# Nine start offsets, 16 bytes apart, for the weight tiles of a two-layer retention and gMLP kernel

## Chip, cores and metric

The kernel runs on one core of one Trainium2 chip. The metric is device time in microseconds of one execution: 906.26 us, the median of three runs of the kernel before (906.09 to 908.04).

## What is computed

Two layers over 512 latent tokens and 256 context tokens, width 1024, all in float32. Layer 0 is a bidirectional multi-scale retention mixer: 4 heads with q and k of 256 and v and z of 512 columns each. Layer 1 is a chunked gMLP with spatial gating: u, v and z of 2048 columns, then an output projection. The latent stream leaves through a final RMSNorm.

```python
def retention_project(h, w_in):
    q = to_heads(h @ w_in[:, :a], RET_HEADS)
    k = to_heads(h @ w_in[:, a:bq], RET_HEADS) * (RET_QK_DIM ** -0.5)
    v = to_heads(h @ w_in[:, bq:cq], RET_HEADS)
    z = h @ w_in[:, cq:]
...
def gmlp_chunk_mixer(h, w_in, vnorm_g, w_s, b_s, w_out):
    u = h @ w_in[:, :GM_WIDTH]
    v = (h @ w_in[:, GM_WIDTH:2 * GM_WIDTH]).astype(F32)
    z = h @ w_in[:, 2 * GM_WIDTH:]
    ...
    y = u * mixed.reshape(b, l, w).astype(u.dtype)
    return (y * jax.nn.silu(z)) @ w_out
```

The change concerns the products `h @ w_in` of both layers and the gMLP's output product.

## The kernel before

**Halves.** Each float32 operand of a large product is split into a high half (the value cast to the type float32r) and a low half (the rest), and a product is three matmuls: low by high, high by low, high by high (`mm3`, L126). `split` (L132) makes the halves: ScalarE casts the high half, VectorE subtracts it from the source for the low half.

**Quads.** A weight block is cut into four quarters, a quad, and the product of a quad takes seven quarter products instead of eight (Strassen-Winograd), with sums of quarters on both sides. `Stream` (L155) holds the list of weight tiles in the order in which they are used. Its `upto` (L195) prepares the next tile two ahead of its use: it takes raw quarters (128 x 1024, loaded by DMA), subtracts where the name begins with T, and splits the result into a tile of halves. `get` hands it to the product.

**Tiles of halves.** `hl_tile` (L110) deals four slots, `hl0` to `hl3`, in turn. A slot is 2080 floats wide, and a tile of halves uses 2048 of them: 1024 of the high half, then 1024 of the low one. The 32 floats (128 bytes) that are left over let a tile begin at byte 0 or at byte 128 of its slot. The rule before is the line

```python
        o = 32 if moves != (i % 2 == 1) else 0
```

where `i` is the slot and `moves` is true for the quads "vz" and "v1". In the program's memory map the slots begin at bytes 138560, 169408, 177728 and 186048 of a partition; modulo 256 that is 64, 192, 64 and 192. So before the change every tile of halves of the quads "kq" and "u", of "o" and of `load_wo` begins at 64 modulo 256, and every tile of "vz" and "v1" at 192. The activations' tiles (`oA..`, `oS..`, `hc`) begin at multiples of 256, and the pieces that a matmul reads lie at multiples of 512 bytes within any of the tiles.

**Two kinds of product.** `features` (L312; quads "kq" and "u") has the weights' halves as the stationary operand and the activations as the moving one, 256 columns; `tokens` (L320; "vz" and "v1") has the activations stationary and the weights' halves moving, 256 columns. `out1` (L1231; blocks "o") has `ya` or `yb` stationary and the weights' halves moving, 512 columns. A quarter product is 24 matmuls; a layer-0 quad is 9 quarter products (seven, and two of the context tokens), a "v1" or "u" quad 7, an "o" block one tile of 24 matmuls.

**Order.** `QUADS` (L255) goes kq 0; vz (0,0) and vz (0,1) side by side; vz (1,0), vz (1,1), kq 1, vz (2,0), vz (2,1), kq 2, vz (3,0), kq 3, vz (3,1). Then come four heads of attention, whose output weights are split by `load_wo` (L873), the four "v1" quads in two pairs, and the eight "u" quads with four "o" blocks behind each of u2, u4, u6 and u7. Two "v1" tiles (the first of v1 0 and of v1 1) are put into the free tiles `oA22` and `oS2` by `place_at` (L273), and bear the name `hl_e` in the trace; they don't pass through `hl_tile`. The order on each engine is the order of the text (`Queue`, with few exceptions); loads are issued by SyncE when a raw slot comes free.

Of the kernel before, what the change touches and what calls it, by code (L numbers as in the profile page):

```python
# [67 lines left out]
def hybrid_kernel(ctx, tc, xT_d, cT_d, cv_d, sv_d, rows_d, ada0_d, adag_d, w_d, rope_d, dec_d, ws_d, id_d, out_d):  # L68
# [13 lines left out]
    def st(shape, tag, dt=F32, bufs=1, name=None):  # L82
        return sb.tile(shape, dt, tag=tag, name=name or tag, bufs=bufs)
# [23 lines left out]
    lay({"w0": 4096, "w1": 4096, "w2": 4096, "w3": 4096, "w7": 4096, "g0": 4096, "g1": 4096, "dec": 4 * TW})  # L107
    hls = [0]

    def hl_tile(moves=False):  # L110

        i = hls[0] % HL
        hls[0] += 1
        t = st([P, 2080], f"hl{i}", F32R, name="hl")
        o = 32 if moves != (i % 2 == 1) else 0
        return t[:, o:o + 2048].rearrange("p (a n) -> p a n", a=2)

    def t2(name, shape=(P, 512), dt=F32):
# [13 lines left out]
    def split(hl, src, late=None):  # L132
        h, l = hl
        act.copy(h, src)
        low = lambda: dve.tensor_tensor(l, src, f32(h), ALU.subtract)
        if late is None:
            low()
        else:
            late.append(low)
# [15 lines left out]
    class Stream:  # L155
# [3 lines left out]
        def __init__(self):  # L159
            self.items, self.loads, self.raws, self.left, self.tiles = [], [], {}, {}, {}  # L160
            self.free, self.stage, self.done, self.sent, self.at = [], 0, 0, 0, -1
            self.gate = self.limit = self.cap = None

        def quad(self, q, names, place=None):
            for name in names:
                self.item(q, name, place)
# [28 lines left out]
        def upto(self, n, late=None):  # L195

            while self.done < min(n, self.limit or len(self.items)):
                q, name, uses, at, place = self.items[self.done]
                self.pump()
                raw = lambda u: self.raws[q, u]  # L200
                r = raw(at)
                if name[0] == "T":
                    dve.tensor_tensor(r, raw(uses[0]), raw(uses[1]), ALU.subtract)
                elif name[0] == "gated":
                    g = self.gate[:, name[1]:name[1] + 512].unsqueeze(1).to_broadcast([P, 2, 512])
                    rr = r.rearrange("p (e n) -> p e n", e=2)
                    dve.tensor_tensor(rr, rr, g, ALU.mult)
                hl = place() if place else hl_tile(q[0] in ("vz", "v1"))
                split((hl[:, 0, :], hl[:, 1, :]), r, late)
                self.tiles[self.done] = hl  # L210
                self.done += 1
                if late is None:
                    self.drop(q, uses)
                else:
                    late.append(lambda: self.drop(q, uses))
# [657 lines left out]
    def load_wo(h):  # L873
        raws = []
        for c in range(4):
            for j in range(len(raws), min(c + 2, 4)):
                raws.append(st([P, 1024], ("w0", "w7")[j % 2], name="raw"))
                load(raws[j], w_d[16 * h + 12 + j])
            if c == 0:
                yield  # L880
            w = hl_tile()
            split((w[:, 0, :], w[:, 1, :]), raws[c])
            wos.setdefault(h, []).append(w)
            yield
# [556 lines left out]
```

## Time and profile before

| what | value |
|---|---|
| three timed runs, us | 906.09, 906.26, 908.04 |
| profiled execution: its span, us (no other time of it is given) | 908.2 |
| mean granted TensorE clock | 0.992 |
| busy TensorE (matmul) / weight load | 884.4 us (97%) / 839.3 us (92%) |
| busy VectorE / ScalarE / GpSimd | 720.0 us (79%) / 445.8 us (49%) / 51.4 us (6%) |
| DMA | 153.81 MB, mean 169 GB/s |

The span is the time from the first to the last instruction of the one execution that was traced. In a row of the timeline stand the start and the length in us, the engine, the operation, its output and inputs by their names in the program, the shape, and how many instructions are merged into the row. Matmuls overlap in the pipeline: a matmul of 256 columns is shown with 0.28 us, but the next one starts after about 0.12 us. The pace, the distance between two starts, is therefore a row's length less the length of one matmul, divided by the count less one.

### The profile page before, as it was taken

To read this page: it belongs to the slowest core of one execution; us is meant where nothing else is said; L and a number is where in the kernel's file an instruction comes from. 1 tells how busy PE (TensorE), PEld (TensorE's weight loads), DVE (VectorE), ACT (ScalarE), POOL (GpSimd) and SP (SyncE) were. 2 spreads that over 40 slices of the span, in tenths; PEclk is the share of its full clock that TensorE was granted. 3 is DMA by queue.
4 is the path that set the end of the run, shared out by engine and by line. 5 is a ranking of instruction groups with operands and counts; after the bars stand their busy time and mean duration, and the time that the engine had idled before them with its cause. 6 is when DMAs were issued, how large, how long until landed. Compare 5 with 4: busy or idle time off the path is not lost.

```text
span 908.2 us, 16915 instructions
## 1 busy us (share of the span) xinstructions
PE 884.4 (97%) x6872; PEld 839.3 (92%) x6872; DVE 720.0 (79%) x1024; ACT 445.8 (49%) x683; POOL 51.4 (6%) x88
## 2 busy tenths in 40 slices
PE   8999999999999999999999999999999999999986
PEld 7899999999999999998989898999999899899875
DVE  3689967698689876888677669999899478689975
ACT  5564634434445435626263558654445444353334
POOL 0001201101101011000000001111000000000000
PEclk9999999999999999999999999999999999999999
DMA  9933957467477458758253611636335035128002
GB/s 338 399 121 109 320 194 255 153 191 223 154 237 239 140 183 316 255 161 260 79 184 118 209 47 59 215 96 211 118 117 187 24 116 187 44 96 283 19 24 93
DMA packets 76782, 153.81 MB, mean 169 GB/s; under 512 B 7840, under 2 KB 34592, under 8 KB 76704
## 3 DMA queue, kind: packets, MB, share of 16 engines
q1 hardware_dynamic: 69840, 130.70, 44.2%
q0 software_dynamic: 6720, 22.03, 6.4%
q8 instruction: 54, 0.88, 0.4%
q14 instruction: 24, 0.20, 0.1%
q10 hardware_dynamic: 144, 0.01, 0.0%
HBM read 128.58 MB, written 24.12 MB: 168 GB/s over the span
## 4 chain that ended last, share of the span: by engine, by line
PE 67%; DVE 19%; DMA 5%; ACT 4%; issue 4%; SPq 1%; DVEq 0%; ACTq 0%
PE pst L54 67%; DVE hl L54 6%; DMA raw<-in_w_dram 3%; DVE raw L54 3%; DVE ya L54 2%; DVE o L54 2%; DVE snap L54 1%; SPq L54 1%; DMA vt<-vt 1%; DMA xq<-in_xT_dram 1%; ACT hl L54 1%; DVE f L54 1%; DVE pf L54 1%; ACT junk L54 1%; DVE oS L54 1%
## 5 line engine op out<-in xcount | busy, mean ns | idle before, releaser
L54 DVE TENSOR_TENSOR hl<-raw,hl 128x1024 fp32r<-128x1024 f32 x195 | 236.0, 1219 | 68.0 <-ACT hl L54 67.8
L54 ACT CAST hl<-raw 128x1024 fp32r<-128x1024 f32 x195 | 203.7, 1050 | 129.0 <-PE pst L54 71.2
L54 PE MATMUL pst<-oS,hl 128*128 128x256 f32 x1104 | 135.6, 282 | 4.6 <-DVE hl L54 3.9
L54 PE MATMUL pst<-hl,oS 128*128 128x256 f32 x1152 | 137.8, 281 | 2.0 <-DVE hl L54 1.8
L54 PEld LDWEIGHTS pst<-hl,oS 128*128 128x128 f32 x1152 | 135.8, 190 | 3.5 <-DVE hl L54 2.3
L54 PEld LDWEIGHTS pst<-oS,hl 128*128 128x128 f32 x1104 | 131.4, 190 | 6.9 <-ACT ya L54 3.7
L54 PE MATMUL pst<-oA,hl 128*128 128x256 f32 x936 | 117.5, 281 | 0.7 <-DVE snap L54 0.5
L54 PEld LDWEIGHTS pst<-oA,hl 128*128 128x128 f32 x936 | 112.2, 189 | 3.2 <-issue 1.3
L54 DVE TENSOR_TENSOR raw<-raw 128x1024 f32<-128x1024 f32 x92 | 111.4, 1218 | 1.2 <-DMA raw<-in_w_dram 0.5
L54 ACT COPY snap<-pst 128x512 f32<-128x512 f32 x92 | 53.9, 586 | 103.4 <-PE pst L54 102.9
L54 PE MATMUL pst<-hl,oA 128*128 128x256 f32 x816 | 98.6, 279 | 0.4 <-DVE snap L54 0.4
L54 PEld LDWEIGHTS pst<-hl,oA 128*128 128x128 f32 x816 | 96.3, 189 | 0.6 <-issue 0.6
L54 PE MATMUL pst<-og,hl 128*128 128x256 f32 x768 | 92.5, 281 | 0.0
L54 PEld LDWEIGHTS pst<-og,hl 128*128 128x128 f32 x768 | 90.4, 189 | 0.9 <-DVE acc L54 0.2
L54 PE MATMUL pst<-hl,ya 128*128 128x512 f32 x288 | 70.8, 399 | 2.7 <-DVE ya L54 2.7
L54 PEld LDWEIGHTS pst<-hl,ya 128*128 128x128 f32 x288 | 54.9, 192 | 15.2 <-DVE ya L54 3.1
L54 PE MATMUL pst<-v,ph 128*128 128x512 f32 x192 | 60.1, 395 | 0.0
L54 DVE TENSOR_TENSOR snap<-pst,snap 128x512 f32<-128x512 f32 x69 | 47.2, 684 | 3.9 <-PE pst L54 3.6
L54 ACT CAST ph<-pf 128x512 fp32r<-128x512 f32 x24 | 14.9, 621 | 67.1 <-DVE pf L54 66.7
L54 PE MATMUL pst<-hl,hc 128*128 128x256 f32 x384 | 47.4, 280 | 0.0
L54 PEld LDWEIGHTS pst<-hl,hc 128*128 128x128 f32 x384 | 46.0, 189 | 0.0
L54 PEld LDWEIGHTS pst<-v,ph 128*128 128x128 f32 x192 | 36.2, 188 | 7.3
(171 smaller groups left out, 970.3 us busy)
## 6 DMA issues: line engine op xcount, KB each, us to landing
raw<-in_w_dram SPq DMA_DIRECT2D x224, 256.0 KB, 4.4
bg<-in_adag_dram SPq DMA_DIRECT2D x32, 512.0 KB, 4.3
ada_w<-in_ada_dram SPq DMA_DIRECT2D x16, 512.0 KB, 8.7
raw<-in_w_dram SPq DMA_DIRECT2D x16, 512.0 KB, 4.3
bg<-in_dec_dram SPq DMA_DIRECT2D x12, 512.0 KB, 4.4
v<-snap POOLq DMA_DIRECT2D x16, 256.0 KB, 5.0
z<-snap POOLq DMA_DIRECT2D x16, 256.0 KB, 4.2
v<-v SPq DMA_DIRECT2D x8, 512.0 KB, 4.3
```

What stands on the lines that cost most here:

```text
L54: made = op(*args, **kw)
```

## The change

`hl_tile` takes another argument, `spread`. Where it is given, the tile begins at `4 * spread % 36` floats into its slot, whatever the slot: 0, 16, 32, 48, 64, 80, 96, 112 or 128 bytes, and then from 0 again. `Stream` numbers the quads and the "o" blocks in the order in which their first tile is prepared (`turn`), and `upto` gives that number. `load_wo` calls `hl_tile` as before, and its tiles and the two `hl_e` tiles keep their places. Kinds, numbers and order of the instructions on each engine are those of before; the addresses alone differ.

```diff
-    def hl_tile(moves=False):
+    def hl_tile(moves=False, spread=None):
...
-        o = 32 if moves != (i % 2 == 1) else 0
+        o = 4 * spread % 36 if spread is not None else 32 if moves != (i % 2 == 1) else 0
...
+            self.turns = {}
+
+        def turn(self, q):
+
+            if q not in self.turns:
+                self.turns[q] = len(self.turns)
+            return self.turns[q]
...
-                hl = place() if place else hl_tile(q[0] in ("vz", "v1"))
+                hl = place() if place else hl_tile(q[0] in ("vz", "v1"), self.turn(q))
```

This gives, by turn:

| quads or blocks in order | bytes into the slot |
|---|---|
| kq 0, vz (0,0), vz (0,1), vz (1,0), vz (1,1), kq 1 | 0, 16, 32, 48, 64, 80 |
| vz (2,0), vz (2,1), kq 2, vz (3,0), kq 3, vz (3,1) | 96, 112, 128, 0, 16, 32 |
| v1 0, v1 1, v1 2, v1 3 | 48, 64, 80, 96 |
| u0, u1, u2, four o | 112, 128, 0, then 16, 32, 48, 64 |
| u3, u4, four o | 80, 96, then 112, 128, 0, 16 |
| u5, u6, four o | 32, 48, then 64, 80, 96, 112 |
| u7, four o | 128, then 0, 16, 32, 48 |

Since the slots begin at 64 or 192 modulo 256 in turn, and the offset no longer evens that out, tiles of one quad now lie at two places modulo 256, 128 bytes apart.

## Prediction

> **What bounds the kernel now.** I read the page's busy line first, then the busy time by stage, then the rows of the timeline in which one kind of matmul runs without a gap.
>
> ```profile
> PE   884.4 (97%) x6872; PEld 839.3 (92%) x6872; DVE 720.0 (79%) x1024; ACT 445.8 (49%) x683; POOL 51.4 (6%) x88
> ```
> ```profile
> 59.80:164.40 104.60, 104.60 (x891) 104.60 (x889) 91.08 (x110) 56.48 (x76) 16.47 (x25) 1.00 0.60 198
> 164.40:345.60 181.20, 179.43 (x1514) 175.73 (x1513) 145.30 (x176) 79.42 (x102) 20.50 (x34) 0.99 0.62 200
> 345.60:550.50 204.90, 202.69 (x1442) 187.69 (x1441) 150.66 (x234) 105.58 (x180) 3.43 (x6) 1.00 0.53 170
> ...
> 558.90:631.50 72.60, 71.95 (x627) 71.36 (x626) 71.22 (x97) 42.01 (x56) 10.07 (x19) 1.00 0.53 177
> 631.50:699.00 67.50, 65.51 (x552) 65.34 (x551) 60.65 (x87) 35.08 (x49) 0.54 (x1) 0.97 0.42 137
> 699.00:908.00 209.00, 197.26 (x1309) 179.48 (x1307) 160.32 (x222) 87.01 (x129) 0.00 (x0) 0.98 0.30 99
> ```
>
> The columns of the second fence are the stretch, its length, then busy time and count of PE, PEld, DVE, ACT and POOL, the granted clock, and DMA. The stages are: the rest of the layer-0 quads up to 345.6 us (at 161.6 begins kq 1), attention, the "v1" quads from 558.9, and the "u" quads and "o" blocks from 631.5. TensorE is busy for 104.60 of 104.60 us, 179.43 of 181.20 and 71.95 of 72.60: in the quads nothing but the pace of the matmuls sets the time. In "v1" VectorE is busy for 71.22 of 72.60 us as well. In the last two stretches the chain that ended last goes through VectorE and DMA too, and TensorE has some 14 us of idle.
>
> A busy TensorE says little; the pace does. These are timeline rows of gapless matmuls:
>
> ```profile
> 84.78 20.42 PE L54 MATMUL pst<-hl,oS 128*128 128x256 f32 x172
> ```
> ```profile
> 285.76 5.60 PE L54 MATMUL pst<-hl,oS 128*128 128x256 f32 x48
> ```
> ```profile
> 550.51 3.04 PE L54 MATMUL pst<-hl_e,oA 128*128 128x256 f32 x24
> ```
> ```profile
> 554.18 3.11 PE L54 MATMUL pst<-hl_e,oA 128*128 128x256 f32 x24
> ```
> ```profile
> 709.82 6.34 PE L54 MATMUL pst<-hl,ya 128*128 128x512 f32 x27
> ```
> ```profile
> 7.93 1.04 PE L54 MATMUL pst<-ident,xq 128*128 128x128 f32 x8
> ```
>
> With one matmul taking 0.28 us (0.39 at 512 columns, 0.27 for the 128-column transposes), the paces are (20.42 - 0.28)/171 = **117.8 ns**, (5.60 - 0.28)/47 = **113.3 ns**, (3.04 - 0.28)/23 = **120.0 ns** and for the second such product (3.11 - 0.28)/23 = 123.0, (6.34 - 0.39)/26 = **228.8 ns** and (1.04 - 0.27)/7 = **110 ns**. The first two rows are the same work at the same start addresses, modulo 256 (weights' halves moving at 192, activations stationary at 0): one stretch goes at 117.8 and another at 113.3, and along the timeline a stretch keeps its pace until TensorE next waits. So there are two steady paces for one arrangement. The third and fourth rows are the only place before where the moving tile and the stationary tile begin at the same place modulo 256 (`hl_e` in `oA22`, `oA11`, both 0), and it goes at 120.0 or more. That is what the change touches: the start of one operand against that of the other. The transposes load 128 columns and move 128; their 110 ns is about what loading alone takes.
>
> **The change part by part.** *Instructions.* None is added, removed or moved, and no wait. The DMAs and their order are the same.
>
> *Writing the tiles.* ScalarE and VectorE write the halves at the new places.
>
> ```profile
> L54 DVE TENSOR_TENSOR hl<-raw,hl 128x1024 fp32r<-128x1024 f32 x195 | 236.0, 1219 | 68.0 <-ACT hl L54 67.8
> L54 ACT CAST hl<-raw 128x1024 fp32r<-128x1024 f32 x195 | 203.7, 1050 | 129.0 <-PE pst L54 71.2
> ...
> L54 DVE TENSOR_TENSOR raw<-raw 128x1024 f32<-128x1024 f32 x92 | 111.4, 1218 | 1.2 <-DMA raw<-in_w_dram 0.5
> ```
>
> The 195 subtractions into slots at two offsets take 1219 ns, those of the raw tiles at quite other places 1218. I take nothing. The trace has no start that is not a multiple of 64 bytes, so this is bounded only by such rows; if each took 2% more, 24 ns by the 179 tiles concerned is 4 us of VectorE, hidden under TensorE except in "v1", where 26 tiles make 0.6 us. A gain I exclude: equal durations at all the present places show nothing left to win.
>
> *Reading the tiles: the term that decides.* By the table of turns, 8 of the 11 layer-0 quads after kq 0 begin off a multiple of 64 (16, 32, 48, 80, 96, 112, 16, 32): 8 x 216 = 1728 matmuls. Of "v1" it is three quads, 3 x 168 less one `hl_e` tile, 480; of "u" five quads (112, 80, 96, 32, 48), 840; of "o" 11 of 16 blocks, 264 matmuls of 512 columns. With offset 64 the tiles in the odd slots begin at 192 + 64 = 256, in step with the other operand, as in the `hl_e` row: some 120 matmuls. That is about 3170 matmuls of 256 columns in a relation that the trace shows at 120.0 or not at all. Bounds from rows: below, 110 ns, where the moving stream costs nothing beside the load; above, an estimate: if an operand is fetched in pieces of 64 bytes, 1024 moved bytes touch 17 pieces instead of 16, and 113.3 x 17/16 = 120.4; 512 loaded bytes touch 9 instead of 8, and 110 x 9/8 = 124. I take **120.0**, the one row in which the relation of the two starts is another than 64 bytes apart; the end of 124 stays for the range.
>
> *The sum*, by stage:
> - vz (0,0), (0,1), (1,0) and half of (1,1), now at 117.8: 750 x 2.2 ns = 1.7 us.
> - turns 5 to 11, of which five quads are off 64: now at either pace, midpoint 115.6: 1080 x 4.4 = 4.8 us. Both on the path (PE 104.60 of 104.60; 179.43 of 181.20).
> - "v1": now at 113.3 nearly throughout. 71.95 us of matmuls of TensorE against 71.22 of VectorE; a slower TensorE leaves VectorE behind it. 510 x 6.7 = 3.4 us.
> - "u": 840 x 4.4 = 3.7, and "o": 264 by an assumed 4.5 ns = 1.2. I count half, 2.5 us, since TensorE waits here for others, and the slower matmuls eat into those waits:
>
> ```profile
> PE pst L54 <- DVE hl L54: 3.9, 3, 2.0
> PE pst L54 <- DVE ya L54: 2.7, 1, 2.7
> PE pst L54 <- DVE snap L54: 0.5, 1, 0.5
> ```
>
> Together 12.4 us. The span becomes 908.2 + 12.4 = 920.6; it lies 1.9 us over the median of the timed runs, so the time is 906.26 + 12.4 = **918.6 us**, +1.4%.
>
> *Clock.* After one wait of TensorE the same 24 matmuls take 4.48 us instead of 2.88 (granted clock 0.97 in that stretch):
>
> ```profile
> 655.73 2.88 PE L54 MATMUL pst<-oS,hl 128*128 128x256 f32 x24
> 660.60 4.48 PE L54 MATMUL pst<-oS,hl 128*128 128x256 f32 x24 [1.99 <-DVE hl L54]
> ```
>
> A wait there that disappears is worth 1.6 us of clock, one that appears costs the same. I put it at 0 plus or minus 3 us.
>
> **The rivals.** *No effect of the place: 906.3, from 901 to 911.* The two paces at one arrangement show that timing after a wait, not address, can choose the pace; then `hl_e` at 120.0 is a third such draw. What is left is that the draws fall differently: 216 matmuls by 4.5 ns is 1.0 us a quad, 4 us if the 104.6 us stretch came out at 113.3. Against it: both `hl_e` products are slower than the slower of the two paces. [...]
>
> *Faster: the collisions are avoided, 886 to 898.* If what lifts the pace above 110 is both streams in one place at the same time, 64 bytes apart may be one of the bad distances, and a finer one may clear it, in half of the slots at least. At 113.3 throughout: 864 x 4.5 = 3.9 us in the first stretch, 1500 x 2.3 = 3.4 in the second, half of 1344 x 2.3 = 1.5 in "u", together 8.8: 897.5. At 110, 3.3 ns more on 2376 + 672 matmuls: 10 us more, 887. "v1" gives nothing, VectorE being busy for 71.22 of 72.60 us. It decides if more than half of the offsets pace below 115.6. For it speaks that 113.3 exists at all; against it, that the three paces seen step up, and none is below 113.
>
> *Much slower, over 930.* Both operands cost a further piece, or the two phases of a quad make TensorE change its pace at each tile: at 126 ns, 3170 x 10.4 = 33 us, 935. Nothing in the trace shows 256-column matmuls above 120 without a wait.
>
> **How the numbers follow.** Forecast (908 to 930, likeliest 918.6): 0.52. Much slower: 0.08. No effect: 0.20, of which 0.06 faster, 0.08 within 0.2%, 0.06 slower. Faster by avoided collisions: 0.20. 0.2% is about what a measurement of this kernel can tell from no change. Slower is 0.52 + 0.08 + 0.06 = 0.66, the same 0.08, faster 0.26. The range 895 to 930 leaves out the 0.08 above and about half of the faster rival.
>
> **What would show it.** In the changed kernel's timeline: vz (0,0) and (0,1), at 59.8 us and later, at 120 or more instead of 117.8; kq 2 and vz (3,0), at offsets 128 and 0, nearer to 113 to 118 than the rest; "v1" clearly longer than 72.6 us with VectorE below 98% of it; VectorE's subtraction at 1219 ns and ScalarE's cast at 1050 unchanged. The forecast falls if quads off 64 bytes run at 113 to 118 as before, and its size is wrong if the paces of neighbouring tiles in one quad differ, since I priced a quad by one pace.

## The result, and the profile after

The changed kernel takes **910.21 us** (median of 16 runs, 906.77 to 912.32) against 906.26 (16 runs, 901.17 to 910.03): ratio **1.0042**, 95% interval 1.0029 to 1.0055. It is slower, as forecast, and inside the range, but by 3.9 us and not by 12.4. The profiled executions are both among the longest of their kernels' runs: the span of before, 908.2, with the 1.8 us that lie around the span after (910.3 in a run of 912.11), would make 910.0, and the longest of its 16 runs took 910.03. Stage lengths of single profiles are therefore read with care below.

The lines of the page that answer to those of before; the first is busy time and count by engine, the others are one group of instructions each, with its mean duration:

```profile
PE 889.3 (98%) x6872; PEld 843.8 (93%) x6872; DVE 720.9 (79%) x1024; ACT 446.3 (49%) x683; POOL 51.5 (6%) x88
...
L54 DVE TENSOR_TENSOR hl<-raw,hl 128x1024 fp32r<-128x1024 f32 x195 | 236.0, 1219 | 69.2 <-ACT hl L54 68.5
L54 ACT CAST hl<-raw 128x1024 fp32r<-128x1024 f32 x195 | 203.7, 1050 | 129.6 <-PE pst L54 72.5
```

VectorE and ScalarE write the halves in 1219 and 1050 ns, as before. TensorE is busy for 4.9 us more. Next the busy time by stage, cut at the same instructions in both kernels (layer-0 quads after kq 0; v1; u and o), with the columns as in the prediction. Before:

```profile
59.81:345.63 285.82, 284.05 (x2403) 280.35 (x2401) 236.37 (x285) 135.92 (x178) 37.00 (x59) 0.99 0.61 199
558.92:631.53 72.61, 71.96 (x628) 71.37 (x626) 71.23 (x97) 41.99 (x56) 10.05 (x19) 1.00 0.53 178
631.53:908.20 276.67, 262.74 (x1858) 244.79 (x1856) 220.94 (x307) 122.09 (x178) 0.54 (x1) 0.98 0.33 108
```

After:

```profile
60.14:348.14 288.00, 286.24 (x2403) 282.51 (x2401) 236.68 (x285) 136.38 (x178) 37.35 (x59) 0.99 0.61 199
561.12:635.17 74.05, 74.03 (x627) 73.81 (x626) 71.82 (x98) 41.98 (x56) 10.01 (x19) 1.00 0.52 175
635.17:910.30 275.13, 263.86 (x1858) 245.18 (x1856) 220.64 (x305) 122.38 (x178) 0.54 (x1) 0.99 0.33 109
```

The quads grow by 2.2 us and v1 by 1.4; u and o are 1.5 us shorter although TensorE is busy there for 1.1 us more. In v1 VectorE falls from 98% to 97% of the stage and TensorE has next to no idle left (74.03 of 74.05 us). The paces, from timeline rows of the changed kernel (vz (0,0) with vz (0,1), then kq 2, then v1):

```profile
83.01 22.94 PE L54 MATMUL pst<-hl,oS 128*128 128x256 f32 x192
```
```profile
251.28 5.60 PE L54 MATMUL pst<-oS,hl 128*128 128x256 f32 x48
```
```profile
567.08 23.02 PE L54 MATMUL pst<-hl,oS 128*128 128x256 f32 x192
```

These are (22.94 - 0.28)/191 = 118.6 ns at offsets 16 and 32, (5.60 - 0.28)/47 = 113.2 at offset 128, and (23.02 - 0.28)/191 = 119.1 at 48 and 64. The shape of the forecast is there, kq 2 fast and the rest slow, but 118.6 stands where it had 120.

### The profile page after: what moved, and what is told of

It is laid out like the page before. It is cut to its first block, busy times and chain, and to the rows that moved or that the text cites. A ratio compares the mean times of both kernels' runs of the same rounds, so it can differ in the third digit from the quotient of the medians.

```text
span 910.3 us, 16915 instructions
## 1 busy us (share of the span) xinstructions
PE 889.3 (98%) x6872; PEld 843.8 (93%) x6872; DVE 720.9 (79%) x1024; ACT 446.3 (49%) x683; POOL 51.5 (6%) x88
## 4 chain that ended last, share of the span: by engine, by line
PE 71%; DVE 16%; DMA 5%; ACT 4%; issue 3%; SPq 0%; DVEq 0%; ACTq 0%
PE pst L54 71%; DVE hl L54 5%; DVE ya L54 3%; DMA raw<-in_w_dram 2%; DVE raw L54 2%; DVE o L54 2%; DMA xq<-in_xT_dram 2%; ACT hl L54 1%; DMA vt<-vt 1%; ACT junk L54 1%; DVE snap L54 1%; DVE pf L54 1%; DVE pl L54 0%; DVE vt L54 0%; ACT ph L54 0%
## 5 line engine op out<-in xcount | busy, mean ns | idle before, releaser
L54 DVE TENSOR_TENSOR hl<-raw,hl 128x1024 fp32r<-128x1024 f32 x195 | 236.0, 1219 | 69.2 <-ACT hl L54 68.5
L54 ACT CAST hl<-raw 128x1024 fp32r<-128x1024 f32 x195 | 203.7, 1050 | 129.6 <-PE pst L54 72.5
L54 PE MATMUL pst<-hl,oS 128*128 128x256 f32 x1152 | 140.2, 282 | 1.8 <-DVE hl L54 1.8
L54 PEld LDWEIGHTS pst<-hl,oS 128*128 128x128 f32 x1152 | 138.3, 190 | 3.0 <-DVE hl L54 2.0
L54 PE MATMUL pst<-oA,hl 128*128 128x256 f32 x936 | 118.2, 281 | 0.2
L54 PE MATMUL pst<-hl,oA 128*128 128x256 f32 x816 | 100.5, 281 | 0.0
L54 PEld LDWEIGHTS pst<-hl,oA 128*128 128x128 f32 x816 | 98.2, 189 | 0.1
```

The lines of the kernel that those rows point to most:

```text
L54: made = op(*args, **kw)
```

## The experiments

Three theories. **Place**: a matmul's pace depends on where one operand begins against the other. **Alternation**: the offset costs nothing, but tiles of one quad at two places, 128 bytes apart, disturb the pace. **Draws**: paces are chosen by timing after a wait, whatever the place.

**map: the disputed cost by itself.** The kernel's body is replaced by rows of 24 matmuls of 256 columns on halves at rest. In the program's memory map both its tiles begin at 128 modulo 256 (bytes 16512 and 25728).

```python
    for role, product in (("m", tokens), ("w", features)):
        for step in range(16):
            o = 4 * step
            w = hl[:, o:o + 2048].rearrange("p (s n) -> p s n", s=2)
            for draw in range(6):
                bank = ps.tile([P, 512], F32, tag="ps", name=role + chr(97 + step), bufs=1)
                product(bank, a, w)
                n = 512 - 32 * draw
                act.copy(res[:, 0:n], bank[:, 0:n])
```

> Leaves the whole computation out: it only multiplies halves at rest, 24 matmuls of 256 columns per row as in a quarter product, the shifted operand moving (ma to mp) or stationary (wa to wp), at starts 0, 16 to 240 bytes from the other operand's modulo 256, six rows of each with a wait for ScalarE between them. Place theory: ma and wa (in step) at 120 ns a matmul in every row; 64 and 192 bytes at 113.3 or 117.8; 128 bytes near 119; starts off a multiple of 64 around 118, spread from 115 to 122. Theory of draws: every start shows the same two or three paces in turn. Theory of alternation (two places within a quad cost, the offset doesn't): every start at 113.3 or 117.8.

The fifth row of each moving case, from the timeline (start, length; `ma` is 0 bytes, each letter 16 more):

```profile
29.54 3.13 PE L54 MATMUL ma<-hl,oa 128*128 128x256 f32 x24 [0.65 <-ACT res L54]
51.98 3.00 PE L54 MATMUL mb<-hl,oa 128*128 128x256 f32 x24 [0.65 <-ACT res L54]
74.26 3.06 PE L54 MATMUL mc<-hl,oa 128*128 128x256 f32 x24 [0.65 <-ACT res L54]
96.79 3.10 PE L54 MATMUL md<-hl,oa 128*128 128x256 f32 x24 [0.65 <-ACT res L54]
119.35 3.09 PE L54 MATMUL me<-hl,oa 128*128 128x256 f32 x24 [0.65 <-ACT res L54]
142.36 3.13 PE L54 MATMUL mf<-hl,oa 128*128 128x256 f32 x24 [0.65 <-ACT res L54]
165.17 3.14 PE L54 MATMUL mg<-hl,oa 128*128 128x256 f32 x24 [0.65 <-ACT res L54]
187.55 3.02 PE L54 MATMUL mh<-hl,oa 128*128 128x256 f32 x24 [0.65 <-ACT res L54]
210.03 3.12 PE L54 MATMUL mi<-hl,oa 128*128 128x256 f32 x24 [0.65 <-ACT res L54]
232.62 3.07 PE L54 MATMUL mj<-hl,oa 128*128 128x256 f32 x24 [0.65 <-ACT res L54]
255.21 3.11 PE L54 MATMUL mk<-hl,oa 128*128 128x256 f32 x24 [0.65 <-ACT res L54]
277.94 3.13 PE L54 MATMUL ml<-hl,oa 128*128 128x256 f32 x24 [0.65 <-ACT res L54]
300.16 2.99 PE L54 MATMUL mm<-hl,oa 128*128 128x256 f32 x24 [0.65 <-ACT res L54]
322.60 3.12 PE L54 MATMUL mn<-hl,oa 128*128 128x256 f32 x24 [0.65 <-ACT res L54]
345.22 3.10 PE L54 MATMUL mo<-hl,oa 128*128 128x256 f32 x24 [0.65 <-ACT res L54]
368.02 3.08 PE L54 MATMUL mp<-hl,oa 128*128 128x256 f32 x24 [0.65 <-ACT res L54]
```

Each row carries the same 0.1 us of starting (its first distance, some 0.22 us), so rows are compared with each other: 2.99 us at 192 bytes, 3.13 in step, nothing outside these by more than 0.01. Without the first two distances the paces are, as median of the six rows, in ns:

| bytes from the other operand | 0 | 16 | 32 | 48 | 64 | 80 | 96 | 112 | 128 | 144 | 160 | 176 | 192 | 208 | 224 | 240 |
|---|---|---|---|---|---|---|---|---|---|---|---|---|---|---|---|---|
| shifted tile moves | 119.5 | 113.3 | 116.8 | 118.4 | 117.8 | 119.8 | 120.1 | 114.6 | 118.7 | 117.7 | 118.6 | 119.4 | 113.3 | 118.8 | 118.2 | 117.1 |
| shifted tile is stationary | 119.5 | 118.4 | 118.3 | 118.0 | 113.3 | 118.7 | 118.6 | 119.8 | 118.6 | 119.6 | 120.1 | 118.1 | 117.8 | 116.7 | 116.7 | 117.4 |

Most places keep one pace through the six rows. Some alternate between two: 16 bytes moving goes at 113.3 in four rows, at 116.9 and 118.6 in the others; 144 moving at 116.6 and 118.8 in turn, so that its 117.7 is the pace of no row; 64 and 192 bytes stationary at 113.3 and 117.8. So each place has paces of its own, and a draw chooses among them. Six rows don't show all of them: 192 moving is at 113.3 in each, and at 117.8 in the first 100 us of the kernel before. The theory of draws alone falls. Of the place theory the sub-rule "off a multiple of 64 is slow" falls too: 16 and 112 bytes moving are among the fastest, and 128, a multiple of 64, is at 118.7.

**alt: two places, no fine offset.**

```diff
-        o = 32 if moves != (i % 2 == 1) else 0
+        o = 0
```

> The kernel before with every tile at byte 0 of its slot: all starts are multiples of 64, tiles lie 64 and 192 bytes from the other operand in turn. Place theory: both relations cost the same (as in the changed kernel, where 64 and 192 both pace at 115), so 906 plus or minus 2 us. Theory of alternation: slower like the changed kernel, 909 to 911.

905.48 us, ratio 0.9996 (0.9976 to 1.0015). Two places in turn, 64 and 192 bytes, cost nothing that can be measured.

**one: the nine offsets, one place per quad.** For this and the next runs the slots all begin at 64 modulo 256: 128 bytes of small tiles are laid ahead of each of `hl1` to `hl3`, and the other large tiles keep their places modulo 256 (some small ones move). The lines are those of the changed kernel:

```diff
-        o = 4 * spread % 36 if spread is not None else 32 if moves != (i % 2 == 1) else 0
+        o = 4 * spread % 36 if spread is not None else 32 if moves else 0
```

> The nine offsets of the change, but in slots that all begin at 64 modulo 256, so that each quad has one relation and not two. Place theory: as the changed kernel, 908 to 913 us, because as many starts are off a multiple of 64. Theory of alternation: back at 906. Theory of draws: 906 plus or minus 4.

910.37 us, ratio 1.0047 (1.0028 to 1.0066): the changed kernel's time without its alternation. With alt, the alternation theory falls.

The two profiles also let the map be tried on the whole kernel. For each layer-0 quad the table has the bytes at which its tiles lie from the other operand, the map's pace for them (the mean over the quad's nine products), and the mean distance between starts in the trace without waits (distances above 0.15 us are left out), in ns. In the pair vz (0,0) and vz (0,1) the tiles go to the slots in turn, so that each of the two keeps one place.

| quad | changed kernel: bytes | map | measured | one: bytes | map | measured |
|---|---|---|---|---|---|---|
| vz (0,0) | 80 | 119.8 | 119.4 | 80 | 119.8 | 119.9 |
| vz (0,1) | 224 | 118.2 | 118.4 | 96 | 120.1 | 120.0 |
| vz (1,0) | 112, 240 | 115.7 | 115.8 | 112 | 114.6 | 113.3 |
| vz (1,1) | 0, 128 | 119.1 | 119.4 | 128 | 118.7 | 118.6 |
| kq 1 | 144, 16 | 119.1 | 118.1 | 144 | 119.6 | 117.0 |
| vz (2,0) | 160, 32 | 117.6 | 117.2 | 160 | 118.6 | 117.3 |
| vz (2,1) | 176, 48 | 119.0 | 118.8 | 176 | 119.4 | 119.2 |
| kq 2 | 192, 64 | 115.3 | 113.4 | 192 | 117.8 | 117.8 |
| vz (3,0) | 64, 192 | 115.8 | 115.4 | 64 | 117.8 | 117.8 |
| kq 3 | 80, 208 | 117.6 | 117.6 | 80 | 118.7 | 118.7 |
| vz (3,1) | 96, 224 | 119.3 | 119.2 | 96 | 120.1 | 120.0 |

Over the eleven quads the map gives 117.9 ns for the changed kernel, and 117.5 was measured; the quads that stand apart from it most (kq 1, kq 2) lie at places of two paces or came out at one that the six rows don't have. In the map the other operand begins at 128 modulo 256, in the kernel at 0. That the paces agree by the distance between the operands therefore also speaks against the rival that the shifted tile's own address modulo 256 sets them.

**half: one bad place for all.** In the even slots:

```diff
-        o = 32 if moves != (i % 2 == 1) else 0
+        o = 16
```

> The same even slots, every tile at byte 64 of its slot, so that all weight tiles lie 128 bytes from the other operand modulo 256; all starts are multiples of 64. Place theory: the changed kernel's tiles with this relation pace at 119.4 ns as moving operand, so some 5000 matmuls lose 3.5 ns, of which the later stages hide part: 914 to 922 us. Theory of draws and theory of alternation: 906 plus or minus 3.

916.52 us (915.19 to 916.82), ratio 1.0113 (1.0094 to 1.0132). A row of vz (1,0) and its neighbours:

```profile
117.65 5.86 PE L54 MATMUL pst<-hl,oS 128*128 128x256 f32 x48
```

(5.86 - 0.28)/47 = 118.7 ns, the map's pace for 128 bytes. In vz (2,0) the same place goes at a second pace, (5.92 - 0.28)/47 = 120.0 ns:

```profile
208.08 5.92 PE L54 MATMUL pst<-hl,oS 128*128 128x256 f32 x48
```

The place theory passes: all these starts are multiples of 64, and the relation alone costs 1.1%.

**ctl, m112, half_q, half_u: the even slots as control, a better place, and one stage at a time.** ctl has the rule before (`o = 32 if moves else 0`) in the even slots. The others replace it (`kind` is the quad's kind, handed to `hl_tile`):

```diff
 m112:   +        o = 12 if moves else 0
 half_q: +        o = 16 if kind in ("kq", "vz") else 32 if moves else 0
 half_u: +        o = 16 if kind in ("u", "o") else 32 if moves else 0
```

> The rule before in the even slots (all slots begin at 64 modulo 256, small tiles moved into the gaps): every tile lies where it lay modulo 256. A control for the next three: 906.4 plus or minus 1.7 us. If it differs, the moved small tiles matter.

> Even slots; the moving tiles of vz and v1 begin 112 bytes from the other operand (48 bytes into the slot) instead of 192, everything else as before. The measured map has that relation at 114.6 ns after every wait, where 192 goes at 113.3 or 117.8. Place theory: some 2350 matmuls gain about 1 ns on the mean, 904 us (902 to 906), with less scatter; a start off a multiple of 64 as such costs nothing. Theory that being off a multiple of 64 costs: 909.

> Even slots; the 128-byte relation (118.7 ns in the map) in the layer-0 quads alone. TensorE has no idle time there, so 2376 matmuls by 118.7 less the mean of 113.3 and 117.8, 3.1 ns, is 7 us: 912 to 915 us if the loss is paid in full, and about 911 if the mean pace of before there is nearer to 117.8 than I think.

> Even slots; the 128-byte relation in the u quads and o blocks alone: 1344 matmuls by 3.1 ns is 4.2 us, and 384 of 512 columns by perhaps 2 ns 0.8 us. Paid in full: 911 us. Half hidden under the waits for VectorE, as the forecast had it: 908 to 909. Wholly hidden: 906.4 plus or minus 1.7.

| run | us (median) | ratio to before | 95% interval |
|---|---|---|---|
| ctl | 905.82 | 0.9970 | 0.9952 to 0.9989 |
| m112 | 903.86 | 0.9951 | 0.9930 to 0.9972 |
| half_q | 912.90 | 1.0057 | 1.0037 to 1.0076 |
| half_u | 906.52 | 0.9997 | 0.9977 to 1.0018 |

The ratios and intervals here and below are those on record, not quotients of the two medians. The control came out 0.3% faster than before, whose runs beside it had a median of 907.80; run again below (ctl2) it is the same. half_q pays: it is 5.1 us slower than before and 7.1 us slower than the control, of the 7 us that were reckoned for a loss paid in full. half_u pays 0.7 us against the control, of 5 reckoned. Its v1 stage, and that of u and o:

```profile
556.34:628.96 72.62, 71.79 (x628) 71.23 (x627) 71.22 (x97) 41.99 (x56) 10.02 (x19) 1.00 0.53 178
628.96:904.60 275.64, 264.56 (x1858) 246.29 (x1856) 221.21 (x307) 121.73 (x178) 0.54 (x1) 1.00 0.33 109
```

TensorE is busy for 264.56 us there against 262.74 before, and the stage is 275.64 us long against 276.67: the slower matmuls took from TensorE's idle time (11.1 us left of 13.9). The stage of before also has stretches at a lower granted clock (0.98 in its row), so the two profiles by themselves only fit what the timed runs say.

m112 is the fastest version seen: 0.5% faster than the runs of the kernel before beside it, and faster than the changed one. Its vz tiles move 112 bytes from the other operand:

```profile
114.30 5.60 PE L54 MATMUL pst<-hl,oS 128*128 128x256 f32 x48
```

(5.60 - 0.28)/47 = 113.2 ns, better than the map's 114.6. The layer-0 quads after kq 0:

```profile
59.47:339.13 279.66, 277.73 (x2402) 273.79 (x2401) 235.53 (x285) 136.11 (x178) 37.37 (x59) 1.00 0.63 204
```

The quads take 279.66 us, against 281.9 in the control's profile. Its runs lie between 901.47 and 904.87, the control's between 903.04 and 908.76; whether a place with one pace scatters less is not shown by 8 runs, as the granted clock scatters them too (0.994 to 0.997 in m112's runs, 0.993 to 0.997 in the control's). Against the control the gain is 2.0 us; these two had no interval of their own, so how much of the 0.5% is the place and how much a favourable sample stays open.

**sp_q, sp_v, sp_u, ctl2: the change in one stage alone.** Against the changed kernel:

```diff
-                hl = place() if place else hl_tile(q[0] in ("vz", "v1"), self.turn(q))
+                hl = place() if place else hl_tile(q[0] in ("vz", "v1"), (None, self.turn(q))[q[0] in ("kq", "vz")])
```

(and `("v1",)`, `("u", "o")`)

> The change in the layer-0 quads alone; v1, u and o lie as before. Forecast's term for this stage: 6.5 us. By the paces of the changed kernel's profile (mean 117.4 ns over these quads against the midpoint 115.6): 2376 x 1.8 = 4.3 us, so 0.4 to 0.5% over the kernel before.

> The change in the v1 quads alone. Forecast's term: 3.4 us. By the two profiles the stage grows from 72.6 to 74.1 us, so 1.4 us where v1 fell on the faster pace before and nothing where it fell on the slower one: 0 to 0.2%.

> The change in the u quads and o blocks alone. Forecast's term: 2.5 us, half of what the matmuls lose. After the run with the 128-byte relation in the same place: nothing that can be measured, below 0.15%.

> The control layout again, beside these three: if its 0.3% against the kernel before was the draw of paces, it is within 0.2% of it now; if moving the small tiles brings something, 0.3% faster again.

| run | us (median) | ratio to before (median 906.30) | 95% interval |
|---|---|---|---|
| sp_q | 909.06 | 1.0032 | 1.0017 to 1.0046 |
| sp_v | 905.22 | 1.0003 | 0.9985 to 1.0021 |
| sp_u | 906.78 | 1.0005 | 0.9986 to 1.0024 |
| ctl2 | 905.82 | 0.9991 | 0.9970 to 1.0011 |

The layer-0 quads alone make 2.9 us of the change's 3.9 (1.5 to 4.2). v1 and the u quads add 0.3 and 0.5 us, neither clear of nothing. The granted clock can't be what makes the changed kernel slower: its mean was 0.997 over that kernel's 16 runs, and 0.995 to 0.996 over the runs of the kernel before that stand beside the experiments.

## Why the prediction was right in direction and wrong in size

*The mechanism* was right in the main: no instruction changed, the writes cost the same, and the place of one operand against the other sets the pace, as map, half, alt and one show. The rule by which it picked the matmuls that pay was wrong. "Off a multiple of 64" is not what is slow: 16 and 112 bytes moving pace at 113.3 and 114.6 ns in the map, and 128 at 118.7, so the estimate by pieces of 64 bytes, an assumption that no run shows, has nothing for it here. The direction was partly luck: the places of before (192 moving, 64 stationary) pace at 113.3, the least that the map has, and nearly any spread would have lost.

The rival "no effect of the place" falls: in the map the pace runs from 113.3 to 120.1 ns with the start of the moving operand, and as far with the start of the stationary one, all 16 starts 16 bytes apart.

*The price was too high*, and this is the step that failed: "I take **120.0**, the one row in which the relation of the two starts is another than 64 bytes apart", set as the pace of every start off a multiple of 64. That row (the operands in step) is one of the slowest places of the map. The others lie between 113.3 and 120.1. No layer-0 quad of the changed kernel reached 120 on the mean; the eight off a multiple of 64 run from 115.8 to 119.4, and those at 128 and 0 at 113.4 and 115.4. Over all layer-0 quads the mean distance between starts, with waits left out, is 117.5 ns after, and 115.3 to 116.6 in the profiles of kernels that have the relation of before. By these means the layer-0 term was 2376 matmuls by some 1.6 ns, 3.8 us, and not 6.5; sp_q measured 2.9.

*"v1", 3.4 us*: the stage was assumed at 113.3 before. That was this profile's draw. With the places of before it took 72.6 us in some profiles and 74.0 in others, and 74.05 after: by these profiles the change costs 1.4 us there or nothing. sp_v measured 0.3 us. The v1 stage of sp_u, where v1 lies as before:

```profile
556.48:630.48 74.00, 73.68 (x627) 73.44 (x626) 71.86 (x98) 41.95 (x56) 10.03 (x19) 1.00 0.52 175
```

*"u" and "o", 2.5 us*: half was counted, nothing clear was paid (sp_u 0.5 us, between -1.3 and 2.2). half_u shows where it goes, into waits, and so do the two profiles of the result. The mean distance of the matmuls of "u" grew there from 115.8 to 117.3 ns and that of "o" from 229.3 to 231.8, 3.0 us in all, while TensorE's idle time in the stage fell from 13.9 to 11.3 us. The step "I count half" named the cover rightly and trusted it too little.

*Clock, 0 plus or minus 3 us*: the profile after has no wait before the matmuls that took 4.48 us before, and they go gapless, at a granted clock of 1.00 and (5.86 - 0.28)/47 = 118.7 ns:

```profile
659.99 5.86 PE L54 MATMUL pst<-oS,hl 128*128 128x256 f32 x48
```

The 1.6 us that are missing there are about what "u" and "o" came out shorter by in this pair of profiles. But the price isn't tied to the wait: in ctl, with the places of before, TensorE waits for 1.77 us at the same instruction, and the 24 matmuls behind it take 3.07 us.

*The three terms together* were 12.4 us; measured one by one they are 2.9 + 0.3 + 0.5 = 3.7, the whole 3.9; with intervals of 1.3 us and more to either side of each, so close a match is partly luck. The forecast added the cost of a slower pace to a profile whose own draw it took for the kernel's: the slow 117.8 of the first 100 us against the fast 113.3 of v1. Both are draws.

*The rival of avoided collisions* was wrong for this change but not idle: a fine offset, 112 bytes for the moving tile, gives the fastest kernel of the study. Its argument against itself, "none is below 113", held: no place of the map has a mean below 113.3, and the 110 ns for loading alone stays an estimate, as no run loads without multiplying.

*What would show it*: vz (0,0) and (0,1) "at 120 or more" is off by the same error of price (118.6). "kq 2 ... nearer to 113" came true (113.2); so did the 1219 and 1050 ns. "v1" at 74.05 us with VectorE at 97% came true too, but shows nothing, since sp_u has 74.00 with the places of before. The sign that the size was wrong, neighbouring tiles of one quad at different paces, came true: in vz (1,0) the tiles at 112 bytes go at 113.3 to 115.3 ns and those at 240 at 116.9 to 117.4.

## What to carry to other kernels

Where TensorE streams without a gap, try the start of the moving tile against that of the stationary one, in 16-byte steps over 256 bytes, in a small kernel that does nothing else, and take a place with one fast pace: 6% lies between the best and the worst here, and mixing places buys their mean. A pace read from a stretch of one profile may be a draw: before pricing its change, see how many paces the same arrangement shows elsewhere in the trace. And here a loss of pace was paid in full only where TensorE has next to no idle time: half_q cost 5 to 7 us in the layer-0 quads (before, TensorE is busy there for 284.05 of 285.82 us), half_u nothing clear in u and o (262.74 of 276.67 us).

## What the runs showed of the hardware that was not expected

In the map the pace of gapless 256-column float32r matmuls with a weight load each depends on the relation of the two operands' starts modulo 256 bytes, in 16-byte steps and without a simple order: with the shifted tile moving, 113.3 ns at 192 bytes and 119.5 at 0, 114.6 at 112 and 120.1 at 96. The map's two rows mirror each other at multiples of 32: moving at 64, 96 or 192 bytes paces as stationary at 192, 160 or 64 (117.8, 120.1, 113.3), within 0.1 ns at all eight. At the odd multiples of 16 they don't (16 moving 113.3, 240 stationary 117.4), so there it also matters which operand is shifted.

In the kernel before one arrangement has two steady paces (113.3 and 117.8 ns), which differ by 4%. The prediction read that a stretch keeps its pace until TensorE next waits. The pace also changes without a wait, at a change of the kind of product. From kq 2 to vz (3,0), it goes from (2.99 - 0.28)/23 = 117.8 to (2.88 - 0.28)/23 = 113.0 ns:

```profile
266.60 2.99 PE L54 MATMUL pst<-oA,hl 128*128 128x256 f32 x24
269.43 2.90 PE L54 MATMUL pst<-hl,oA 128*128 128x256 f32 x24
272.17 2.88 PE L54 MATMUL pst<-hl,hc 128*128 128x256 f32 x24
```

The kernel before ranged from 901.17 to 910.03 us over 16 runs, and the two paces are only part of that. Of its 83 runs beside the experiments, the 18 with a mean granted clock of 0.994 or less took 909.2 us on the mean and the 26 with 0.997 or more 905.6. Why a place has its pace, and what chooses between two, no run here tells.
